# Products of 128x256 pieces: ordered by width in the FFN, and two-column-block products with halves summed in the projections

## The chip, the cores and the metric

The kernel runs on one core of a Trainium2 chip, in one launch. The metric is the device time of that launch in microseconds (us). Before the change it is 1240.27 us, the median of three runs (1240.12 to 1240.30).

## What is computed

The input x is 256 tokens by 1024 features in float32. Two models run one after the other on it, each of depth two:

```
x = x + gmlp_mixer(x);            x = x + swiglu_ffn(x)      # first_block, layer 0
x = x + chunked_attention(x);     x = x + swiglu_ffn(x)      # layer 1: 16 heads, relative bias
x = rms_norm(x)
for l in range(2):                                          # second_block
    p = rms_norm(x) @ w_in[l]                               # 2832 columns
    y = concat(conv31(p), attention4(p), gated_linear_attention(p)) @ w_out[l]
    x = x + y
    u = conv3(rms_norm(x) @ ffn_w_up[l])
    x = x + (silu(u[:, :2816]) * u[:, 2816:]) @ ffn_w_down[l]
x = rms_norm(x)
```

All weights are float32 and are read from memory once. The matrix products are made from pairs of a rounded high part and a low part: a product h @ w is hi(h)·hi(w) + lo(h)·hi(w) + hi(h)·lo(w).

## The kernel before

**Staging.** SP's queue brings the weights in tiles of 128x2048 (`raw`). For each half of such a tile ScalarE (ACT) writes the high part `wh` (L105) and VectorE (DVE) the low part `wl` (L116, or L118 where a gain is multiplied in). `take` hands such pairs to the products in the order of the stream, `release` gives them back, `pump` splits the next ones ahead of their use, up to eight. The activations lie transposed in `hT`, of shape 128 x 8 x 2 x 256: for each of the eight feature blocks k the high part of all 256 tokens and behind it the low part, so that `hT[2][:, k]` is one operand of 512 columns.

**Pieces.** A piece is a product of 128 output features with all 256 tokens: the weight block is the stationary operand, the tokens stream. There are two ways to make one:

- narrow (`mmB`, L350 to L352): 24 products of 256 columns, all into one half of a PSUM bank: for each k wh with hi, wh with lo, wl with hi. `mmB2` makes two pieces into the two halves of one bank. The reader takes the bank directly.
- wide (`mmB_wide`, L363 and L366): eight products of 512 columns (wh with hi and lo side by side, into the two halves of one bank) and eight of 256 columns (wl with hi, into the first half), alternately; the last two change places. The piece is then the sum of the bank's halves: ACT copies the second half out (L634), DVE adds the first (L636).

The four FFNs use the wide form for pieces 2 to 21 of both halves of the up projection (2 x 20 in each FFN). The gMLP groups (16 pieces), the attention's k and q (16), and in each of the two mixers the conv inputs (4), two q/k pairs (4), the gated attention's q (2) and k (2) use the narrow form. The other products are `mmA` (tokens stationary, L339) and `down` (L393 to L395), all 512 columns wide but for one of 272.

**Order.** Only SP's order is written out by hand; on the other engines a scheduler places the instructions of each engine by the program's order and its own estimates, and the order is then fixed. PSUM has eight banks in one pool, of which `down` holds four while it accumulates. In the mixer the 60 taps of the 31-wide convolution (L958, DVE, 128x256 each) are background work: `step` puts a few behind each `pump`. The mixer's `kd` and `kg` (L1063, L1064) are DVE products of the k pieces with decays; PE transposes `kd` (L1080) and multiplies `kg` (L1113) between the products of `gate(0)`. In attention, step s makes k and q of s (`project`, copied out at L858 and L859), and PE's scores (L746) use them one step later, for the first step one product later.

Of the kernel before, what the change touches and what calls it, by code (L numbers as in the profile page):

```python
# [150 lines left out]
class Net:  # L151
# [192 lines left out]
    def mmB(self, out, hT, w):  # L344

        mm = self.nc.tensor.matmul
        vh = w[0].rearrange("p (k n) -> p k n", n=P)
        vl = w[1].rearrange("p (k n) -> p k n", n=P)
        for k in range(KD):
            mm(out, lhsT=vh[:, k, :], rhs=hT[0][:, k, :], start=(k == 0), stop=False)  # L350
            mm(out, lhsT=vh[:, k, :], rhs=hT[1][:, k, :], start=False, stop=False)  # L351
            mm(out, lhsT=vl[:, k, :], rhs=hT[0][:, k, :], start=False, stop=(k == KD - 1))  # L352

    def mmB_wide(self, hT, w):


        mm = self.nc.tensor.matmul
        ps = self.mm([P, 2, S])
        vh = w[0].rearrange("p (k n) -> p k n", n=P)
        vl = w[1].rearrange("p (k n) -> p k n", n=P)  # L360

        def wide(k):
            mm(ps, lhsT=vh[:, k, :], rhs=hT[2][:, k], start=(k == 0), stop=(k == KD - 1))  # L363

        def low(k):
            mm(ps[:, 0, :], lhsT=vl[:, k, :], rhs=hT[0][:, k, :], start=False, stop=False)  # L366

        for k in range(KD):
            for f in (wide, low) if k < KD - 1 else (low, wide):
                f(k)  # L370
        return ps

    def mmB2(self, hT, name="mm"):

        ids, ws = self.ws.take(2)
        ps = self.mm([P, 2, S], name)
        for j in range(2):
            self.mmB(ps[:, j, :], hT, ws[j])
        self.ws.release(ids)
        return ps  # L380
# [239 lines left out]
    def ffn(self, hT, fin, next_gains, conv=None, final=False):  # L620
        nc = self.nc
        with self.tc.tile_pool(name="ff", bufs=1) as pool:
            self.ws.ext(pool, DEFER)
            acts = {}

            wide = True
# [54 lines left out]
            for i in range(2, NPAIR):  # L681
                if wide:
                    ids, ws = self.ws.take(2)
                    ps = [self.mmB_wide(hT, w) for w in ws]
                    self.ws.release(ids)
                else:
                    ps = self.mmB2(hT)
# [101 lines left out]
    def attention(self, hTs, fin, second, next_gains):  # L789
        nc = self.nc  # L790
        hkv, hq = hTs
        with self.tc.tile_pool(name="at", bufs=1) as pool:
# [25 lines left out]
            def project(s, ws, ps, which):  # L818
                self.mmB(ps[:, which, :], (hq, hkv)[which], ws)
# [24 lines left out]
            for s in range(8):  # L844
                ids, ws = self.ws.take(2)
                ps = self.mm([P, 2, S])
                project(s, ws[0], ps, 1)
# [7 lines left out]
                project(s, ws[1], ps, 0)  # L855
                self.ws.release(ids)
                qk = pool.tile([P, 2, S], F32, tag="qk", name="qk", bufs=2)
# [41 lines left out]
    def mixer(self, l, hT, fin, next_gains):  # L899
# [5 lines left out]
        with self.tc.tile_pool(name="mx", bufs=1) as pool:  # L905
# [100 lines left out]
            ids, ws = self.ws.take(2)  # L1006
            ps = self.mm([P, 2, S])
            self.mmB(ps[:, 0, :], hT, ws[0])
            lg = self.mm([P, 2, S], "lg")
            for t in range(2):  # L1010
                nc.tensor.matmul(lg[:, t, :], lhsT=gT[:, t * P : (t + 1) * P], rhs=gw,
                                 start=True, stop=True)
            la = big([P, 2, S], "la")
            last = nc.scalar.activation(la, lg, AF.Abs)
            with self.tc.issue_after(last.ins):
                ld = nc.scalar.preload_act_table_set("natural_log_exp_and_others")
            with self.tc.issue_after(ld.ins):
                nc.scalar.activation(la, la, AF.Exp, scale=-1.0)
            nc.scalar.activation(la, la, AF.Ln, bias=1.0)
            nc.vector.scalar_tensor_tensor(la, lg, 0.0, la, op0=ALU.min, op1=ALU.subtract)  # L1020
            self.mmB(ps[:, 1, :], hT, ws[1])
            self.ws.release(ids)
            qk_out(ps)
            step(2, TAPS[4])
            qk_out(self.mmB2(hT))
# [5 lines left out]
            ids, ws = self.ws.take(2)  # L1031
            qps = self.mm([P, 2, S])
            self.mmB(qps[:, 0, :], hT, ws[0])
            gts = []
            for m in (tri, aft):
                gt = self.mm([P, 2, S], "gt")
                for s in range(2):
                    for t in range(2):
                        nc.tensor.matmul(gt[:, s, t * P : (t + 1) * P],
                                         lhsT=la[:, t, s * P : (s + 1) * P], rhs=m,  # L1040
                                         start=True, stop=True)
                gts.append(gt)
# [3 lines left out]
            nc.scalar.activation(eG, gts[0], AF.Exp)  # L1046
            nc.scalar.activation(enG, gts[0], AF.Exp, scale=-1.0)
            nc.scalar.activation(kdx, gts[1], AF.Exp)
            self.mmB(qps[:, 1, :], hT, ws[1])
            self.ws.release(ids)  # L1050
# [11 lines left out]
            ps = self.mmB2(hT)  # L1062
            nc.vector.tensor_mul(kd, ps, kdx)  # L1063
            nc.vector.tensor_mul(kg, ps, enG)  # L1064
# [437 lines left out]
```

## Time and profile before

| | before |
|---|---|
| median of three runs | 1240.27 us |
| the profiled execution: its time | 1240.27 us |
| the profiled execution: its span | 1238.5 us |
| mean granted TensorE clock | 0.999 of 2.4 GHz |
| TensorE matmul (PE) busy | 1228.8 us, 7160 instructions |
| VectorE (DVE) busy | 903.5 us |
| ScalarE (ACT) busy | 715.1 us |

The span is the time from the first to the last instruction; 1.8 us of the execution lie around it. PE's rows start when a product starts; their ends are modelled, so neighbouring products overlap in the records, and what a product costs in a stream is the distance from its start to the start of the next. PEld is the load of a stationary operand, which runs beside the product ahead of it.

### The profile page before, as it was taken

What the parts mean: (1) busy time and instruction counts of PE and PEld (TensorE: products, weight loads), DVE (VectorE), ACT (ScalarE), POOL (GpSimd) and SP (SyncE); (2) the same over time, 40 slices, a digit from 0 to 9 for tenths busy, and PEclk for the clock granted to TensorE, in tenths of its full rate; (3) what the DMA queues carried; (4) which work ended last, traced back from release to release, by engine and by line L of the source; (5) the groups of instructions that cost most, each with busy time, mean ns of one, the idle gap of its engine ahead of it and who ended that gap; (6) DMA issues with size and microseconds to landing.
All of it is one profiled execution on the core that took longest, in us unless ns stands there. A gap on an engine that the chain in (4) does not pass through costs nothing.

```text
span 1238.5 us, 18456 instructions
## 1 busy us (share of the span) xinstructions
PE 1228.8 (99%) x7160; PEld 1055.0 (85%) x7160; DVE 903.5 (73%) x1497; ACT 715.1 (58%) x1237; POOL 41.3 (3%) x95
## 2 busy tenths in 40 slices
PE   9999999999999999999999999999999999999997
PEld 7899888888888888888889878888888978888886
DVE  6676676766567757676669867979885977889874
ACT  7644465655456546565546556667663745767653
POOL 1100000000000000000010010000001011000000
PEclk9999999999999999999999999999999999999999
DMA  8854465675444435567524345557542425566720
GB/s 290 307 201 170 153 210 199 209 267 192 148 161 171 163 134 206 183 238 246 184 103 170 120 155 203 171 187 278 198 170 86 164 75 216 182 221 216 252 71 34
DMA packets 34827, 226.14 MB, mean 183 GB/s; under 512 B 4242, under 2 KB 4660, under 8 KB 9140
## 3 DMA queue, kind: packets, MB, share of 16 engines
q1 hardware_dynamic: 34596, 224.97, 51.7%
q8 instruction: 56, 0.92, 0.3%
q14 instruction: 31, 0.25, 0.1%
q10 hardware_dynamic: 144, 0.00, 0.0%
HBM read 223.91 MB, written 1.05 MB: 182 GB/s over the span
## 4 chain that ended last, share of the span: by engine, by line
PE 97%; DVE 2%; ACT 1%; POOL 0%; issue 0%; POOLq 0%; ACTq 0%
PE mm L363 24%; PE mm L339 12%; PE mm L366 12%; PE acc L393 9%; PE acc L395 9%; PE acc L394 9%; PE mm L350 5%; PE mm L351 4%; PE mm L352 4%; PE tr L239 1%; PE sc L746 1%; PE mm L497 1%; PE pt L777 1%; PE sp L578 1%; PE po L835 1%; PE po L1202 0%
## 5 line engine op out<-in xcount | busy, mean ns | idle before, releaser
L116 DVE TENSOR_TENSOR wl<-raw,wh 128x1024 fp32r<-128x1024 f32 x378 | 458.8, 1223 | 201.0 <-ACT wh L105 200.1
L105 ACT ACTIVATE wh<-raw 128x1024 fp32r<-128x1024 f32 x378 | 395.1, 1055 | 246.1 <-PE mm L363 89.5
L363 PE MATMUL mm<-hT,wh 128*128 128x512 f32 x1280 | 452.1, 397 | 0.0
L366 PE MATMUL mm<-hT,wl 128*128 128x256 f32 x1280 | 333.2, 281 | 0.0
L363 PEld LDWEIGHTS mm<-hT,wh 128*128 128x128 f32 x1280 | 235.2, 188 | 46.2
L366 PEld LDWEIGHTS mm<-hT,wl 128*128 128x128 f32 x1280 | 241.6, 189 | 14.2
L339 PE MATMUL mm<-wh,hT 128*128 128x512 f32 (+1 forms) x480 | 149.1, 383 | 0.0
L350 PE MATMUL mm<-hT,wh 128*128 128x256 f32 x448 | 128.9, 288 | 0.0
L351 PE MATMUL mm<-hT,wh 128*128 128x256 f32 x448 | 126.8, 283 | 0.1
L352 PE MATMUL mm<-hT,wl 128*128 128x256 f32 x448 | 126.6, 283 | 0.0
L393 PE MATMUL acc<-wh,ah 128*128 128x512 f32 x320 | 125.6, 393 | 0.0
L395 PE MATMUL acc<-wh,al 128*128 128x512 f32 x320 | 124.5, 389 | 0.0
L394 PE MATMUL acc<-wl,ah 128*128 128x512 f32 x320 | 124.5, 389 | 0.0
L339 PEld LDWEIGHTS mm<-wh,hT 128*128 128x128 f32 x480 | 86.8, 188 | 16.8 <-issue 1.1
L350 PEld LDWEIGHTS mm<-hT,wh 128*128 128x128 f32 x448 | 85.7, 191 | 5.5 <-issue 5.2
L339 PE MATMUL mm<-wl,hT 128*128 128x512 f32 (+1 forms) x240 | 90.2, 381 | 0.0
L351 PEld LDWEIGHTS mm<-hT,wh 128*128 128x128 f32 x448 | 85.8, 192 | 0.7 <-DVE hT L233 0.5
L352 PEld LDWEIGHTS mm<-hT,wl 128*128 128x128 f32 x448 | 85.8, 191 | 0.0
L636 DVE TENSOR_TENSOR sum<-mm,sum 128x256 f32<-128x256 f32 x160 | 66.6, 419 | 15.1 <-ACT sum L634 15.0
L651 DVE SCALAR_TENSOR_TENSOR gu<-sum,prm,gu 128x255 f32<-128x255 f32 (+1 forms) x160 | 72.7, 480 | 5.4 <-ACT gu L646 3.5
L634 ACT ACTIVATE sum<-mm 128x256 f32<-128x256 f32 x160 | 58.8, 369 | 31.1 <-PE mm L363 30.7
L394 PEld LDWEIGHTS acc<-wl,ah 128*128 128x128 f32 x320 | 60.2, 188 | 13.0
(221 smaller groups left out, 1458.5 us busy)
## 6 DMA issues: line engine op xcount, KB each, us to landing
raw<-in_w_ffn SPq DMA_DIRECT2D x66, 1024.0 KB, 4.9
raw<-in_w_up SPq DMA_DIRECT2D x66, 1024.0 KB, 4.9
raw<-in_w_mix SPq DMA_DIRECT2D x30, 1024.0 KB, 4.9
raw<-in_w_gmlp SPq DMA_DIRECT2D x22, 1024.0 KB, 5.1
raw<-in_w_att SPq DMA_DIRECT2D x16, 1024.0 KB, 4.9
raw<-in_w_gmlp SPq DMA_DIRECT2D x4, 512.0 KB, 6.2
bias<-in_rel SPq DMA_DIRECT2D x8, 256.0 KB, 3.9
x<-in_x SPq DMA_DIRECT2D x4, 256.0 KB, 5.4
```

What stands on the lines that cost most here:

```text
L105: self.nc.scalar.activation(hi, r, AF.Copy, scale=1.0 if g is None else g)
L116: self.nc.vector.tensor_sub(lo, r, hi.bitcast(F32))
L339: mm(out, lhsT=hT[a][:, k, ts], rhs=view(b, k), start=(i == 0), stop=(i == 3 * KD - 1))
L350: mm(out, lhsT=vh[:, k, :], rhs=hT[0][:, k, :], start=(k == 0), stop=False)
L351: mm(out, lhsT=vh[:, k, :], rhs=hT[1][:, k, :], start=False, stop=False)
L352: mm(out, lhsT=vl[:, k, :], rhs=hT[0][:, k, :], start=False, stop=(k == KD - 1))
L363: mm(ps, lhsT=vh[:, k, :], rhs=hT[2][:, k], start=(k == 0), stop=(k == KD - 1))
L366: mm(ps[:, 0, :], lhsT=vl[:, k, :], rhs=hT[0][:, k, :], start=False, stop=False)
L393: mm(acc, lhsT=act[0][:, ts], rhs=w[0][:, c], start=(first and i == 0), stop=False)
L394: mm(acc, lhsT=act[0][:, ts], rhs=w[1][:, c], start=False, stop=False)
L395: mm(acc, lhsT=act[1][:, ts], rhs=w[0][:, c], start=False, stop=(last and i == n - 1))
L651: nc.vector.scalar_tensor_tensor(gu[:, j, d:], ps[:, j, : S - d], ws3[j][2 - d], gu[:, j, d:], op0=ALU.mult, op1=ALU.add,)
```

## The change

The wide form no longer alternates: it makes seven products of 512 columns, then the eight of 256, then the last of 512. The narrow form and `mmB2` are gone; all 56 pieces that used them are wide now, and two new functions sum the halves into an SBUF tile, with a scale where q is scaled. What read the bank before reads that tile. `qk` in attention has three buffers for two. In the mixers the work that stood between two narrow pieces (`logits`, `decays`) is passed as `mid` and stands at the same place.

```diff
     def mmB_wide(self, hT, w):
-        for k in range(KD):
-            for f in (wide, low) if k < KD - 1 else (low, wide):
-                f(k)
+        for k in range(KD - 1):
+            wide(k)
+        for k in range(KD):
+            low(k)
+        wide(KD - 1)
         return ps
 
-    def mmB2(self, hT, name="mm"):
+    def half_sum(self, ps, out, scale=1.0):
+        self.nc.scalar.activation(out, ps[:, 1, :], AF.Copy, scale=scale)
+        if scale == 1.0:
+            self.nc.vector.tensor_add(out, ps[:, 0, :], out)
+        else:
+            self.nc.vector.scalar_tensor_tensor(out, ps[:, 0, :], scale, out,
+                                                op0=ALU.mult, op1=ALU.add)
+
+    def mmB_sum(self, hT, outs, scales=(1.0, 1.0), mid=None):
         ids, ws = self.ws.take(2)
-        ps = self.mm([P, 2, S], name)
         for j in range(2):
-            self.mmB(ps[:, j, :], hT, ws[j])
+            if j == 1 and mid is not None:
+                mid()
+            self.half_sum(self.mmB_wide(hT, ws[j]), outs[j], scales[j])
         self.ws.release(ids)
...
# gMLP, group(g)
-                ps = self.mmB2(hT)
-                nc.vector.tensor_mul(u, ps, rrow[:, None, :].to_broadcast([P, 2, S]))
+                self.mmB_sum(hT, [u[:, j, :] for j in range(2)])
+                nc.vector.tensor_mul(u, u, rrow[:, None, :].to_broadcast([P, 2, S]))
...
# attention, step s
-            def project(s, ws, ps, which):
-                self.mmB(ps[:, which, :], (hq, hkv)[which], ws)
+            def project(ws, qk, which):
+                self.half_sum(self.mmB_wide((hq, hkv)[which], ws), qk[:, which, :],
+                              (0.125, 1.0)[which])
...
-                nc.scalar.activation(qk[:, 0, :], ps[:, 0, :], AF.Copy, scale=0.125)
-                nc.vector.tensor_copy(qk[:, 1, :], ps[:, 1, :])
...
# mixer
             def conv_in(s):
-                ps = self.mmB2(hT)
-                nc.scalar.activation(th, ps[:, 1, :], AF.Tanh, scale=0.5)
-                nc.vector.scalar_tensor_tensor(hpad[:, s, 30:], th, 1.0, ps[:, 0, :],
-                                               op0=ALU.add, op1=ALU.mult)
+                c = hpad[:, s, 30:]
+                self.mmB_sum(hT, [c, th])
+                nc.scalar.activation(th, th, AF.Tanh, scale=0.5)
+                nc.vector.scalar_tensor_tensor(c, th, 1.0, c, op0=ALU.add, op1=ALU.mult)
...
-            def qk_out(ps):
+            def qk_out(mid=None):
                 qk = big([P, 2, S], "qk")
-                nc.scalar.activation(qk[:, 0, :], ps[:, 0, :], AF.Copy, scale=0.125)
-                nc.scalar.activation(qk[:, 1, :], ps[:, 1, :], AF.Copy)
+                self.mmB_sum(hT, [qk[:, j, :] for j in range(2)], (0.125, 1.0), mid)
...
-            nc.vector.scalar_tensor_tensor(qg, qps, 0.125, eG, op0=ALU.mult, op1=ALU.mult)
+            self.mmB_sum(hT, [qg[:, j, :] for j in range(2)], (0.125, 0.125), decays)
+            nc.vector.tensor_mul(qg, qg, eG)
...
-            ps = self.mmB2(hT)
-            nc.vector.tensor_mul(kd, ps, kdx)
-            nc.vector.tensor_mul(kg, ps, enG)
+            self.mmB_sum(hT, [kg[:, j, :] for j in range(2)])
+            nc.vector.tensor_mul(kd, kg, kdx)
+            nc.vector.tensor_mul(kg, kg, enG)
```

How the instructions stand on their engines is shown at three places. In each row stand the line, the operation, what is written and read, the shape, and a count where a row repeats.

The first place is PE in the first FFN, behind the `down` products of a step: two pieces. Before (L363 is the wide product, L366 the low one):

```order
L395 MATMUL acc_1717<-wh,al 128x512
L363 MATMUL mm<-hT,wh 128x512
L366 MATMUL mm<-hT,wl 128x256
L363 MATMUL mm<-hT,wh 128x512
L366 MATMUL mm<-hT,wl 128x256
L363 MATMUL mm<-hT,wh 128x512
L366 MATMUL mm<-hT,wl 128x256 x2
L363 MATMUL mm<-hT,wh 128x512 x2
L366 MATMUL mm<-hT,wl 128x256
```

After the change (L354 is the wide product, L357 the low one, L397 the last of `down`):

```order
L397 MATMUL acc_1629<-wh,al 128x512
L354 MATMUL mm<-hT,wh 128x512 x7
L357 MATMUL mm<-hT,wl 128x256 x8
L354 MATMUL mm<-hT,wh 128x512 x8
L357 MATMUL mm<-hT,wl 128x256 x8
L354 MATMUL mm<-hT,wh 128x512
```

The widths change fourteen times inside a piece before and twice after; the last wide product of the first piece joins the seven of the second.

The second place is DVE in the first mixer, around `kd` and `kg` (L958 and L953 are the taps, L370 the sum of halves). Before:

```order
L958 SCALAR_TENSOR_TENSOR cy<-hpad,prm,cy 128x256 x2
L116 TENSOR_TENSOR wl<-raw,wh 128x1024
L958 SCALAR_TENSOR_TENSOR cy<-hpad,prm,cy 128x256 x2
L118 SCALAR_TENSOR_TENSOR wl<-raw,misc,wh 128x1024
L958 SCALAR_TENSOR_TENSOR cy<-hpad,prm,cy 128x256 x2
L1063 TENSOR_TENSOR kd<-mm,kdx 128x512
L1064 TENSOR_TENSOR kg<-mm,enG 128x512
```

After:

```order
L953 SCALAR_TENSOR_TENSOR cy<-hpad,prm,cy 128x256 x4
L116 TENSOR_TENSOR wl<-raw,wh 128x1024
L370 TENSOR_TENSOR kg<-mm,kg 128x256
L953 SCALAR_TENSOR_TENSOR cy<-hpad,prm,cy 128x256 x2
L116 TENSOR_TENSOR wl<-raw,wh 128x1024
L370 TENSOR_TENSOR kg<-mm,kg 128x256
L953 SCALAR_TENSOR_TENSOR cy<-hpad,prm,cy 128x256
L1054 TENSOR_TENSOR kd<-kg,kdx 128x512
L953 SCALAR_TENSOR_TENSOR cy<-hpad,prm,cy 128x256
L1055 TENSOR_TENSOR kg<-kg,enG 128x512
L118 SCALAR_TENSOR_TENSOR wl<-raw,misc,wh 128x1024
```

Two sums now stand ahead of `kd` here, and the last gained split has moved behind `kg`. From the second conv gate (L966 before, L962 after) to `kg` there are on DVE 51 taps and 12 splits before, and 50 taps, 11 splits and eight sums after.

The third place is PE at the start of the first mixer, where the first conv piece needs the last part of `hT` (names with their buffer numbers; `mm_6160` is the first conv piece before, `mm_5969` after). Before:

```order
L239 MATMUL tr_6146<-ident_101,hn_6098 128x128 x4
L339 MATMUL mm_6117<-wh_5904,hT_6038 128x512
L350 MATMUL mm_6160<-hT_6038,wh_5907 128x256
L350 MATMUL mm_6224<-hT_6038,wh_6213 128x256
L351 MATMUL mm_6160<-hT_6038,wh_5907 128x256
L352 MATMUL mm_6160<-hT_6038,wl_5908 128x256
```

After:

```order
L239 MATMUL tr_5954<-ident_101,hn_5906 128x128 x4
L339 MATMUL mm_5925<-wh_5712,hT_5846 128x512
L354 MATMUL mm_5969<-hT_5846,wh_5715 128x512 x4
L354 MATMUL mm_5988<-hT_5846,wh_5745 128x512
L354 MATMUL mm_5969<-hT_5846,wh_5715 128x512 x3
L357 MATMUL mm_5969<-hT_5846,wl_5716 128x256 x8
```

Two products that read the high part alone stood first; now the first product reads high and low parts together.

## Rows read from the trace of the kernel before

**Rows 1.** The page: busy us, share and instructions of each engine; the chain's shares.
```profile
PE 1228.8 (99%) x7160; PEld 1055.0 (85%) x7160; DVE 903.5 (73%) x1497; ACT 715.1 (58%) x1237; POOL 41.3 (3%) x95
...
PE 97%; DVE 2%; ACT 1%; POOL 0%; issue 0%; POOLq 0%; ACTq 0%
```

**Rows 2.** Waits of PE, the longest: waiter, releaser, us in total, times, longest.
```profile
PE warm L423 <- POOL ident masks.py:199: 1.4, 1, 1.4
```

**Rows 3.** Groups by line: count | busy us, mean ns | idle before.
```profile
L363 PE MATMUL mm<-hT,wh 128*128 128x512 f32 x1280 | 452.1, 397 | 0.0
...
L350 PE MATMUL mm<-hT,wh 128*128 128x256 f32 x448 | 128.9, 288 | 0.0
```

**Rows 4.** Timeline of PE, first FFN: start us, duration us, line, operands, count.
```profile
295.57 0.39 PE L363 MATMUL mm<-hT,wh 128*128 128x512 f32 x1
...
300.97 0.40 PE L363 MATMUL mm<-hT,wh 128*128 128x512 f32 x1
301.21 0.40 PE L393 MATMUL acc<-wh,ah 128*128 128x512 f32 x1
...
301.67 0.39 PE L395 MATMUL acc<-wh,al 128*128 128x512 f32 x1
...
303.93 0.39 PE L363 MATMUL mm<-hT,wh 128*128 128x512 f32 x1
```

**Rows 5.** Timeline of PE, a gMLP group: first narrow product, and what follows 48.
```profile
79.39 0.28 PE L350 MATMUL mm<-hT,wh 128*128 128x256 f32 x1
...
85.14 0.72 PE L578 MATMUL sp<-wsT,v 128*128 128x128 f32 x5
```

**Rows 6.** Timeline of PE, first mixer: 512-column products behind a run of 272.
```profile
664.18 0.40 PE L339 MATMUL mm<-wl,hT 128*128 128x512 f32 x1
...
666.03 0.39 PE L339 MATMUL mm<-wl,hT 128*128 128x512 f32 x1
```

**Rows 7.** Groups by line: a weight split, and the two steps of a sum.
```profile
L116 DVE TENSOR_TENSOR wl<-raw,wh 128x1024 fp32r<-128x1024 f32 x378 | 458.8, 1223 | 201.0 <-ACT wh L105 200.1
...
L636 DVE TENSOR_TENSOR sum<-mm,sum 128x256 f32<-128x256 f32 x160 | 66.6, 419 | 15.1 <-ACT sum L634 15.0
...
L634 ACT ACTIVATE sum<-mm 128x256 f32<-128x256 f32 x160 | 58.8, 369 | 31.1 <-PE mm L363 30.7
```

**Rows 8.** Busy us by stretch: length, then PE, PEld, DVE, ACT, POOL.
```profile
53.00:152.00 99.00, 99.00 (x656) 90.95 (x656) 66.59 (x78) 47.11 (x61) 1.95 (x5) 1.00 0.52 180
361.00:426.00 65.00, 65.00 (x539) 58.68 (x538) 48.74 (x138) 41.54 (x99) 1.59 (x8) 1.00 0.50 180
...
655.00:705.00 50.00, 50.00 (x373) 46.04 (x373) 48.95 (x104) 32.83 (x59) 0.00 (x0) 1.00 0.50 170
```

**Rows 9.** Tile uvh, gMLP: durations min/median/max ns, first and last start.
```profile
L393 PE MATMUL acc<-wh,uvh x64: 389/389/477, 73.8 to 151.1; 128*128 128x512 f32 x64
...
L232 ACT ACTIVATE uvh<-u x8: 631/633/634, 64.7 to 137.2; 128x512 fp32r<-128x512 f32 x8
```

**Rows 10.** Timeline of all engines, first mixer: the first conv piece and its wait.
```profile
645.80 0.69 DVE L233 TENSOR_TENSOR hT<-tr,hT 128x512 fp32r<-128x512 f32 x1
...
646.10 0.40 PE L350 MATMUL mm<-hT,wh 128*128 128x256 f32 x2
646.54 0.19 PEld L351 LDWEIGHTS mm<-hT,wh 128*128 128x128 f32 x1 [0.26 <-DVE hT L233]
```

**Rows 11.** Timelines of DVE and PE, attention: first step's copy, and its scores.
```profile
370.63 0.42 DVE L859 COPY qk<-mm 128x256 f32<-128x256 f32 x1
...
371.28 0.49 PE L746 MATMUL sc<-qk 64*128 64x128 f32 x4
```

**Rows 12.** Timeline of DVE, first mixer: eleven taps, and kg.
```profile
660.67 4.57 DVE L958 SCALAR_TENSOR_TENSOR cy<-hpad,prm,cy 128x256 f32<-128x256 f32 x11
...
698.70 0.70 DVE L1064 TENSOR_TENSOR kg<-mm,enG 128x512 f32<-128x512 f32 x1
```

**Rows 13.** Timeline of PE, first mixer: where kg is first read.
```profile
703.07 0.72 PE L1113 MATMUL at<-qg,kg 64*128 64x128 f32 x8
```

More of the change, by code (lines that the diff above doesn't have):

```diff
@@ L342, in mmA @@
                     f()
[L344 to L348, printed above, removed]
-        for k in range(KD):
-            mm(out, lhsT=vh[:, k, :], rhs=hT[0][:, k, :], start=(k == 0), stop=False)
-            mm(out, lhsT=vh[:, k, :], rhs=hT[1][:, k, :], start=False, stop=False)
-            mm(out, lhsT=vl[:, k, :], rhs=hT[0][:, k, :], start=False, stop=(k == KD - 1))
     def mmB_wide(self, hT, w):
@@ L624, in ffn @@
             acts = {}
-            wide = True
             def finish(i, ps):
@@ L681, in ffn @@
             for i in range(2, NPAIR):
[L682 to L686, printed above, removed]
-                    ps = self.mmB2(hT)
+                ids, ws = self.ws.take(2)
+                ps = [self.mmB_wide(hT, w) for w in ws]
+                self.ws.release(ids)
                 if i == 2:
@@ L845, in attention @@
                 ids, ws = self.ws.take(2)
-                ps = self.mm([P, 2, S])
-                project(s, ws[0], ps, 1)
+                qk = pool.tile([P, 2, S], F32, tag="qk", name="qk", bufs=3)
+                project(ws[0], qk, 1)
                 if s >= 2:
@@ L854, in attention @@
                     load_bias(s + 3)
-                project(s, ws[1], ps, 0)
+                project(ws[1], qk, 0)
                 self.ws.release(ids)
-                qk = pool.tile([P, 2, S], F32, tag="qk", name="qk", bufs=2)
-                nc.scalar.activation(qk[:, 0, :], ps[:, 0, :], AF.Copy, scale=0.125)
-                nc.vector.tensor_copy(qk[:, 1, :], ps[:, 1, :])
                 qks[s] = qk
@@ L998, in mixer @@
             qks = []
-            def qk_out(ps):
+            def qk_out(mid=None):
                 qk = big([P, 2, S], "qk")
-                nc.scalar.activation(qk[:, 0, :], ps[:, 0, :], AF.Copy, scale=0.125)
-                nc.scalar.activation(qk[:, 1, :], ps[:, 1, :], AF.Copy)
+                self.mmB_sum(hT, [qk[:, j, :] for j in range(2)], (0.125, 1.0), mid)
                 qks.append(qk)
-            ids, ws = self.ws.take(2)
-            ps = self.mm([P, 2, S])
-            self.mmB(ps[:, 0, :], hT, ws[0])
@@ L1009, in mixer @@
[L1009 to L1012, printed above, removed]
-            la = big([P, 2, S], "la")
[L1014 to L1023, printed above, removed]
+            la = big([P, 2, S], "la")
+            def logits():
+                lg = self.mm([P, 2, S], "lg")
+                for t in range(2):
+                    nc.tensor.matmul(lg[:, t, :], lhsT=gT[:, t * P : (t + 1) * P], rhs=gw,
+                                     start=True, stop=True)
+                last = nc.scalar.activation(la, lg, AF.Abs)
+                with self.tc.issue_after(last.ins):
+                    ld = nc.scalar.preload_act_table_set("natural_log_exp_and_others")
+                with self.tc.issue_after(ld.ins):
+                    nc.scalar.activation(la, la, AF.Exp, scale=-1.0)
+                nc.scalar.activation(la, la, AF.Ln, bias=1.0)
+                nc.vector.scalar_tensor_tensor(la, lg, 0.0, la, op0=ALU.min, op1=ALU.subtract)
@@ L1024, in mixer @@
+            qk_out(logits)
             step(2, TAPS[4])
-            qk_out(self.mmB2(hT))
+            qk_out()
             sm0, sums0 = self.sm_scores(pool, qks[0], [caus, caus], False, 4)
             step(2, TAPS[5])
[L1031 to L1042, printed above, removed]
@@ L1045, in mixer, with decays @@
             kdx = big([P, 2, S], "kdx")
[L1046 to L1050, printed above, removed]
+            def decays():
+                gts = []
+                for m in (tri, aft):
+                    gt = self.mm([P, 2, S], "gt")
+                    for s in range(2):
+                        for t in range(2):
+                            nc.tensor.matmul(gt[:, s, t * P : (t + 1) * P],
+                                             lhsT=la[:, t, s * P : (s + 1) * P], rhs=m,
+                                             start=True, stop=True)
+                    gts.append(gt)
+                nc.scalar.activation(eG, gts[0], AF.Exp)
+                nc.scalar.activation(enG, gts[0], AF.Exp, scale=-1.0)
+                nc.scalar.activation(kdx, gts[1], AF.Exp)
             qg = big([P, 2, S], "qg")
+            self.mmB_sum(hT, [qg[:, j, :] for j in range(2)], (0.125, 0.125), decays)
             kg = big([P, 2, S], "kg")
             kd = big([P, 2, S], "kd")
-            nc.vector.scalar_tensor_tensor(qg, qps, 0.125, eG, op0=ALU.mult, op1=ALU.mult)
+            nc.vector.tensor_mul(qg, qg, eG)
             sm1, sums1 = self.sm_scores(pool, qks[1], [caus, caus], False, 4)
```

2 lines of the change are left out of this document (removed).

## The prediction, made before the change was run

> **What bounds the kernel now.** I began with the page: PE is busy for 1228.8 us of a span of 1238.5 and makes 97% of the chain, while DVE and ACT work 73% and 58% of the span [rows 1]. The view of waits then has PE's largest wait, 1.4 us, at the warm-up at the start; the others come to less than 2 us together [rows 2]. So PE is the bound from one end to the other, and at full clock (mean granted clock 0.999 of 2.4 GHz). The time can only fall if the same products take PE less time, and it can only rise if PE begins to wait. Busy sums don't show the first, since their durations (397 ns for a product of 512 columns, 288 for one of 256, [rows 3]) overlap. What counts is the distance from one start to the next, and for that I read the timeline of PE.
>
> - A stream of 512: from 301.67 to 303.93 lie ten products of `down`, 2.26 us, 226 ns each [rows 4].
> - A stream of 256: 48 products in 79.39 to 85.14, 5.75 us, 119.8 ns each. That is a pair of narrow pieces, so one narrow piece is 2.875 us [rows 5].
> - The alternating piece: two of them run from 295.57 to 301.21, so one is 2.82 us [rows 4].
>
> Eight products of 512 and eight of 256 at their streams' distances would be 8 x 0.226 + 8 x 0.1198 = 2.766 us. The alternating piece thus pays about 0.054 us for its fourteen changes of width, and the narrow one pays 0.109 us for having 24 products where 16 would do. These two excesses are all that the change can win.
>
> **The piece after the change.** It has two changes of width, and the eight wide products come in one run behind each run of eight low ones. What remains of the 0.054 us has to be bounded. If each change costs alike, 2/14 of it stays: 0.007 us, a piece of 2.773. But the rows say that a run of 512 starts slowly behind narrower products: the three from 300.97 to 301.67, which follow two low products, take 0.70 us where 3 x 0.226 is 0.678, so 0.022 more [rows 4]; and in the first mixer eight products of 512 behind a run of 272-column ones take 1.85 us where 8 x 0.226 is 1.808, 0.042 more [rows 6]. Ends: 0.007 and 0.042. I take 0.022, because those rows hold the very products of this piece, a wide one behind low ones. The piece is then 2.788 us, between 2.773 and 2.808.
>
> **The FFNs.** 1280 wide products by eight are 160 pieces [rows 3]. Each gains 2.82 − 2.788 = 0.032 us: 5.1 us, with ends of 1.9 (0.012 each) and 7.5 (0.047 each). No engine gets more work there, and the sums come at the same place.
>
> **The projections.** 448 products in L350, by eight, are 56 narrow pieces [rows 3]. Each gains 2.875 − 2.788 = 0.087 us: 4.9 us, with ends of 3.8 (0.067) and 5.7 (0.102).
>
> The Trainium skill, on its page "TensorE: Matmul & The Clock Gate", section "Back-to-back issue gap", gives for isolated products one cycle of 2.4 GHz per column and a fixed 2.5 ns: 216 ns for 512 columns and 109 for 256. By it order is worth nothing, and dropping eight of 24 products saves 20 ns a piece, 1.1 us in all as an estimate. The trace differs, with 226 and 119.8 ns [rows 4, 5], and the measurement decides.
>
> **What the sums add.** Each of the 56 pieces now needs a copy on ACT, 0.369 us, and a sum on DVE, 0.419 us [rows 7]. Eight sums take the place of copies, so DVE gets 48 x 0.42 = 20 us and ACT, where 16 copies fall away, 40 x 0.37 = 15 us. Both are off PE's path as long as they have room: in the gMLP DVE works 66.6 of 99 us, in the attention 48.7 of 65 [rows 8]. In the gMLP the gated product is written from 64.7 on and first read by `down` at 73.8 [rows 9]; a cover of 8 us and more hides a sum of 0.8 us. Cost nothing; with the cover gone it would be those 0.8 us once per group. The gMLP's other `take`s and the queues of SP and POOL keep their rows, so no transfer moves.
>
> **Three places where a reader is close behind.**
>
> First, the start of each mixer. DVE writes the last low part of `hT` at 645.80; PE makes two products that need only the high part at 646.10, and the next, which needs the low one, starts at 646.54 [rows 10]. The first wide product needs both, so the two products, 0.24 us at 119.8 each, no longer fill the wait. Twice: 0.5 us. The ends are 0 (something else fills it) and 1.4 (the write comes later by its own length, 0.69 us, in either mixer).
>
> Second, attention's first step: DVE's copy of k starts at 370.63, and the scores start at 371.28 [rows 11]. The copy's place is taken by ACT's copy and DVE's sum, 0.79 for 0.42, while the one or two pieces ahead of it end 0.087 us earlier each. I take 0.1 us; the ends are 0 and one split of 1.2 [rows 7], if one queues ahead. The other steps read a whole step later and hide it.
>
> Third, `kd` and `kg` in the mixers, where DVE has no idle time: 48.95 us of 50 busy [rows 8]. What stands ahead of `kg` changes from 51 taps and 12 splits to 50 taps, 11 splits and eight sums. A tap is 4.57 / 11 = 0.42 us [rows 12], a split 1.22 [rows 7]: 8 x 0.42 − 0.42 − 1.22 = 1.72 us later. `kg` starts at 698.70 and takes 0.70 [rows 12], so it would end at 701.1. PE first reads it at 703.07 [rows 13]; twelve projection pieces ahead of it gain 12 x 0.087 and the first place gives 0.24 back, so PE wants it at 702.3. That leaves 1.2 us of the 3.7 there are now. Cost 0; as it stands close, the end is 1.4 per mixer, a split and a bit more than the slack taken away.
>
> **The sum.** 5.1 + 4.9 − 0.5 − 0.1 = 9.4 us. The profiled execution itself took 1240.27 us, which is the median of the three runs: 1240.27 − 9.4 = 1230.9. I say 1231.0.
>
> **The rivals.**
>
> *The run-in costs its full price.* Each run of wide products behind low ones costs 0.042 us as behind the 272s [rows 6]. Then the FFNs win 1.9 and the projections 3.8, less 0.6: 1235.2 us. For it: those are eight products in a row, as many as a run after the change. Against: the narrower products there are another line and another width. Chance 0.12.
>
> *DVE becomes the bound in front of `kg`.* If DVE is more than 1.2 us later than worked out, by a split more ahead of `kd`, PE waits for `kg`, and each us beyond costs one in either mixer. Up to two splits, 2.4 us, twice: up to 1236, some 1233.5 in the middle. For it: DVE has hardly a gap there [rows 8]. Against: taps can step back, and the rows were counted in the order itself. Chance 0.09.
>
> *Columns alone count.* All forms have 6144 columns a piece: eight by 512 and eight by 256, or 24 by 256. If PE's time went by columns, nothing would be won and 0.6 us lost: 1240.9. Against it: 226 / 512 is 0.441 ns a column, 119.8 / 256 is 0.468 [rows 4, 5]; and the two forms differ by 0.055 us a piece. Chance 0.02. The page named above comes near to this with a time of about 1239.8, as an estimate.
>
> *Banks come back late: slower.* A wide piece takes a bank of its own, where a pair of narrow ones shared one, and it is free only when ACT has copied and DVE has summed. In the attention a step then uses seven banks of the eight where it used six. If a sum stands behind a split, the bank is held 0.37 + 1.22 + 0.42 = 2.0 us longer [rows 7]. Should PE wait that long in each of the eight steps, it loses 16 us, and the time is 1247; with the first five of them the gain is gone. For it: DVE is 75% busy in this stage [rows 8]. Against: the FFNs give banks back in just this way for 160 pieces, and no wait of PE there reaches 1.4 us [rows 2]. Chance 0.04.
>
> That the change doesn't do what it says is nearly excluded, as the order of PE has seven, eight and one in the FFN and in the mixer.
>
> **How the numbers follow.** The forecast has 0.73, the four rivals 0.12, 0.09, 0.02 and 0.04. The range: below, both gains at their upper ends, 7.5 + 5.7 − 0.6 = 12.6, 1227.7 us; above, the run-in at its full price, 1235.2, set at 1235.4 for what the first place may cost more; it takes in most of the second rival. Outside lie the last two rivals, the worst of the second and a few hundredths below. About 0.2%, 2.5 us, is what a measurement of this kernel can tell from no change, so faster means below 1237.8. The forecast and the first two rivals are faster, 0.94, less 0.01 for a sum of misfortunes: 0.93. The same is 0.03 (columns alone, and the edge of the last rival), slower 0.04.
>
> **What the profile after would show.** The FFN: two pieces from the first wide product to the first of `down` in 5.58 us for 5.64, with the 0.022 in the first two or three wide products of each run; if two pieces take 5.62, the first rival holds. The projections: a pair in 5.58 us for 5.75. PE's waits: new rows of 0.2 to 0.3 us at the first conv piece, for `hT` from DVE; a row at `kg` (L1104 or near) for the second rival; a row at a wide product of the attention, for a bank freed by a sum, for the last. DVE's load between 655 and 705 stays full and ACT's rises. The prediction is wrong if the wide products in runs are not at 226 ns, or if PE's waits grow past 3 us.

## The result and the profile after

The changed kernel takes 1233.22 us, the median of six runs (1232.45 to 1233.95), against 1240.14 for the kernel before, measured beside it (1240.12 to 1240.30, six runs). The ratio is 0.9944 with a 95% interval of 0.9934 to 0.9954: 6.9 us less, where 9.4 were forecast. The profiled execution took 1232.47 us, at the lower edge of the six; against the profiled execution of before it is 7.8 us shorter. So two things are to be explained: 1.6 us between the gain that was forecast and the gain of this execution, and another 0.75 between this execution and the median. The second has its own sign: the times of before lie within 0.2 us, those of the changed kernel within 1.5.

The page of the changed kernel, its first part, answers to [rows 1]; below it PE's waits, which answer to [rows 2] (engine and line, what it waited for, us in total, times, longest):

```profile
PE 1220.2 (99%) x6712; PEld 1031.3 (84%) x6712; DVE 918.9 (75%) x1545; ACT 727.6 (59%) x1277; POOL 41.6 (3%) x95
```

```profile
PE warm L425 <- POOL ident masks.py:199: 1.4, 1, 1.4
PE mm L499 <- DVE wl L116: 0.9, 2, 0.5
PE mm L354 <- DVE hT L233: 0.6, 2, 0.3
PE tr L239 <- DMA x<-in_x: 0.3, 1, 0.3
PE tr L239 <- DVE hn L221: 0.3, 1, 0.3
PE acc L395 <- ACT ah L232: 0.2, 1, 0.2
```

PE is still the bound: 8.6 us less busy, 448 products fewer, DVE 15.4 and ACT 12.5 us more. One row is new, the first wide product of each mixer behind `hT`, 0.3 us twice, as the prediction said. No wait for a bank in the attention and none at `kd` or `kg` is to be seen in this execution. One sign failed: between 655 and 705 us DVE stays full (49.55 of 50 us), but ACT's load did not rise (32.30 us for 32.83; the same stretch, with a mixer that begins 4.6 us earlier).

The timeline of PE in the first FFN and in a gMLP group (start, duration, line, operands, count) answers to [rows 4] and [rows 5]; L395 to L397 are `down`:

```profile
293.33 1.75 PE L354 MATMUL mm<-hT,wh 128*128 128x512 f32 x7
294.92 1.11 PE L357 MATMUL mm<-hT,wl 128*128 128x256 f32 x8
295.87 2.00 PE L354 MATMUL mm<-hT,wh 128*128 128x512 f32 x8
297.71 1.12 PE L357 MATMUL mm<-hT,wl 128*128 128x256 f32 x8
298.67 0.40 PE L354 MATMUL mm<-hT,wh 128*128 128x512 f32 x1
298.90 0.40 PE L395 MATMUL acc<-wh,ah 128*128 128x512 f32 x1
...
301.64 1.07 PE L354 MATMUL mm<-hT,wh 128*128 128x512 f32 x4
```

```profile
78.90 1.75 PE L354 MATMUL mm<-hT,wh 128*128 128x512 f32 x7
...
84.47 1.05 PE L580 MATMUL sp<-wsT,v 128*128 128x128 f32 x8
```

Two FFN pieces take 298.90 - 293.33 = 5.57 us, for 5.64 before; but the twelve `down` products behind them take 301.64 - 298.90 = 2.74, for 2.72 before (301.21 to 303.93 in [rows 4]). A pair of pieces with its `down` thus went from 8.36 to 8.31; the means over 72 such pairs, by the nanosecond starts in the traces, are 8.363 and 8.313. A pair in the gMLP takes 5.57 us, for 5.75.

The same product of PE, looked up in both timelines at the border of each stage, gives what every stage won, in us (a worked table, not rows of a view):

```
stage          gMLP  FFN 1  attention  FFN 2  mixer 1  FFN 3  mixer 2  FFN 4  sum
expected       1.4   1.3    1.3        1.3    0.8      1.3    0.8      1.3    9.4
measured       1.5   1.0    1.1        1.0    0.6      1.1    0.65     1.05   8.0
```

The four FFNs gave 4.1 us for the 5.1 expected, the projections 3.9 for 4.3; 0.2 of the 8.0 is given back in the tail behind the last product.

### The profile page after: what moved, and what is told of

The parts are those of the page before. It is cut to its first block, busy times and chain, and to the rows that moved or that the text cites. A ratio compares the mean times of both kernels' runs of the same rounds, so it can differ in the third digit from the quotient of the medians.

```text
span 1230.7 us, 17579 instructions
## 1 busy us (share of the span) xinstructions
PE 1220.2 (99%) x6712; PEld 1031.3 (84%) x6712; DVE 918.9 (75%) x1545; ACT 727.6 (59%) x1277; POOL 41.6 (3%) x95
## 4 chain that ended last, share of the span: by engine, by line
PE 97%; DVE 2%; ACT 1%; POOL 0%; issue 0%; POOLq 0%; ACTq 0%
PE mm L354 32%; PE mm L357 17%; PE mm L339 12%; PE acc L395 9%; PE acc L397 9%; PE acc L396 9%; PE tr L239 1%; PE sc L743 1%; PE mm L499 1%; PE pt L774 1%; PE sp L580 1%; PE po L833 1%; PE po L1193 0%; PE dS L1081 0%; PE po L1189 0%; ACT sq L196 0%
## 5 line engine op out<-in xcount | busy, mean ns | idle before, releaser
L354 PE MATMUL mm<-hT,wh 128*128 128x512 f32 x1728 | 452.7, 393 | 0.6 <-DVE hT L233 0.6
L354 PEld LDWEIGHTS mm<-hT,wh 128*128 128x128 f32 x1728 | 315.9, 189 | 61.9 <-issue 5.2
L357 PEld LDWEIGHTS mm<-hT,wl 128*128 128x128 f32 x1728 | 235.7, 190 | 17.0
L357 PE MATMUL mm<-hT,wl 128*128 128x256 f32 x1728 | 240.9, 282 | 0.0
L395 PE MATMUL acc<-wh,ah 128*128 128x512 f32 x320 | 126.0, 394 | 0.0
L397 PE MATMUL acc<-wh,al 128*128 128x512 f32 x320 | 124.9, 390 | 0.0
L397 PEld LDWEIGHTS acc<-wh,al 128*128 128x128 f32 x320 | 60.1, 188 | 13.5
L395 PEld LDWEIGHTS acc<-wh,ah 128*128 128x128 f32 x320 | 60.4, 189 | 10.0 <-issue 0.3
L646 ACT ACTIVATE gu<-sum,prm 128x256 f32<-128x256 f32 x80 | 46.5, 594 | 19.9 <-DVE sum L636 19.9
L339 PEld LDWEIGHTS mm<-wl,hT 128*128 128x128 f32 x240 | 45.1, 188 | 9.3 <-issue 1.1
L953 DVE SCALAR_TENSOR_TENSOR cy<-hpad,prm,cy 128x256 f32<-128x256 f32 x120 | 52.0, 485 | 0.3
L660 ACT ACTIVATE sg<-sum 128x256 f32<-128x256 f32 x40 | 16.6, 416 | 40.8 <-DVE sum L636 40.8
```

The costliest lines, as they stand in the source:

```text
L339: mm(out, lhsT=hT[a][:, k, ts], rhs=view(b, k), start=(i == 0), stop=(i == 3 * KD - 1))
L395: mm(acc, lhsT=act[0][:, ts], rhs=w[0][:, c], start=(first and i == 0), stop=False)
L397: mm(acc, lhsT=act[1][:, ts], rhs=w[0][:, c], start=False, stop=(last and i == n - 1))
L953: nc.vector.scalar_tensor_tensor(y[:, s, :], hpad[:, s, j : j + S], prm[:, w : w + 1], y[:, s, :], op0=ALU.mult, op1=ALU.add)
```

## The experiments

**Control.** The changed kernel once more.

> The changed kernel once more. Its six times so far lie between 1232.45 and 1233.95 us, while the six of the kernel before lie within 0.2 us; the profiled one of them, 1232.47, is at the lower edge. Theory: the spread of 1.5 us is at some place that only some executions pass through, so the median stays near 1233.2 and the lowest near 1232.4; if the profile of this run is one of the longer ones, the distance between its products and those of the first profile shows the place. Rival: the spread is of that one chip or session, and the times here agree within 0.3 us.

Five runs: 1232.54 median, 1232.32 to 1234.03, ratio 0.9942 (0.9929 to 0.9954). The spread is there again, and this run's profile fell on a short execution.

**The order alone.** The kernel before with

```diff
-        for k in range(KD):
-            for f in (wide, low) if k < KD - 1 else (low, wide):
-                f(k)
+        for k in range(KD - 1):
+            wide(k)
+        for k in range(KD):
+            low(k)
+        wide(KD - 1)
```

> Only the order in the FFN's 160 wide pieces is changed; the 56 narrow pieces stay as before. Theory: a run of wide products behind low ones costs 27 ns more than its stream, of which the first low products behind it give 7 back, so an ordered piece takes 2.793 us and gains 0.027: 4.3 us, a time of 1235.9 (1235.4 to 1236.3). An FFN step of six pieces and two groups of down goes from 25.08 to 24.92 us. Rival, the prediction's 0.032 a piece: 5.1 us, 1235.1, and a step of 24.89. Rival, only columns count: 1240.2.

1236.08 us (1236.01 to 1236.13), ratio 0.9968 (0.9955 to 0.9980): a gain of 4.0 us, no spread. That is 80 pairs by the 0.05 us of the timeline, and it is well below the 5.1 of the prediction. The expectation's own term, 0.027 us a piece or 4.3 us, was a little high too.

**The sums alone.** The changed kernel, but its FFN makes its pieces with a copy of the alternating function of before:

```diff
...
-                ps = [self.mmB_wide(hT, w) for w in ws]
+                ps = [self.mmB_alt(hT, w) for w in ws]
```

> Only the 56 projection pieces become wide ones with sums, in the new order; the FFN alternates as before. Theory: 0.087 us a piece, 4.9, less 0.6 at the start of each mixer and of the attention: a gain of 4.2, a time of about 1236.0 (1235.5 to 1236.8), with no wait of PE but two of about 0.3 us for hT in the mixers. The gains of this run and of the run with the order alone add up to that of the whole change. Rival, DVE late for kg: a wait of PE at the line that reads kg and a gain under 3.

1236.79 us median of eight runs, 1236.46 to 1238.11, ratio 0.9974 (0.9963 to 0.9984). By the shortest execution the gain is 3.6 us, and 4.0 + 3.6 = 7.6 is what the changed kernel wins in its own short executions (7.5 to 7.8): the two parts add up. By the median it is 3.3. The spread of 1.65 us comes with this part. The execution that was profiled is the longest, 1238.11, and it has a wait of PE at `kg`, as the rival expected, and one at `kd`, in the first mixer. Waits of PE in that stretch:

```profile
PE tr L1088 <- DVE kd L1071: 0.5, 1, 0.5
PE at L1121 <- ACT wh L105: 0.4, 1, 0.4
```

Its timelines of ACT and DVE there (in brackets the idle time before, and what ended it):

```profile
692.97 1.15 ACT L105 ACTIVATE wh<-raw,misc 128x1024 fp32r<-128x1024 f32 x1 [2.69 <-DMA raw<-in_w_mix]
...
695.40 0.36 ACT L385 ACTIVATE kg<-mm 128x256 f32<-128x256 f32 x1
```

```profile
695.79 0.42 DVE L387 TENSOR_TENSOR kg<-mm,kg 128x256 f32<-128x256 f32 x1 [1.82 <-ACT kg L385]
...
699.17 0.68 DVE L1071 TENSOR_TENSOR kd<-kg,kdx 128x512 f32<-128x512 f32 x1
```

Read from the top: ACT stands for 2.69 us at a weight split whose tile has not landed. The copy of the first k piece's half is behind it, comes at 695.40, and DVE, idle for 1.82 us, can sum only then. So `kd` is late, and PE waits. Set beside the control's starts from the beginning of the mixer on, PE falls behind by 0.62 us at `kd`, 0.56 at `kg` and 0.34 at a product further on that reads the state which DVE updates (L1210): 1.5 us in this mixer, of the 1.65 by which the execution is longer than the shortest. The view names a split of ACT as what ended the wait at L1121; what that product reads is `kg`, which DVE writes right behind `kd`.

**A look for a long execution of the changed kernel itself**, three single runs of it.

> The changed kernel, one execution with its profile. Theory: an execution over 1233 us shows in the first or second mixer a weight tile that lands late, ACT waiting over 2 us for it with the copy of a k piece's half behind it, and PE waiting for kd and at kg for what is over 1.2 us of that; one under 1232.8 shows no such wait. Rival: a long execution has its extra time elsewhere.

> The same as the run before it: if over 1233 us, the extra time stands at kd and kg in a mixer; if under 1232.8, nowhere.

> The same again: if over 1233 us, the extra time stands at kd and kg in a mixer; if under 1232.8, nowhere.

They took 1232.99, 1232.49 and 1232.38 us. The first is half a us longer than the second, and its products stand level with those of the control's short execution from the first products on (within 0.05 us, and 0.02 in the first mixer) until PE comes to `kg` there. There they part. ACT in the control and then in the long one, the same split and the same copy:

```profile
688.52 1.15 ACT L105 ACTIVATE wh<-raw,misc 128x1024 fp32r<-128x1024 f32 x1 [0.35 <-DMA raw<-in_w_mix]
...
690.95 0.36 ACT L368 ACTIVATE kg<-mm 128x256 f32<-128x256 f32 x1
```

```profile
689.85 1.15 ACT L105 ACTIVATE wh<-raw,misc 128x1024 fp32r<-128x1024 f32 x1 [1.67 <-DMA raw<-in_w_mix]
...
692.27 0.36 ACT L368 ACTIVATE kg<-mm 128x256 f32<-128x256 f32 x1
```

and `kg` on DVE with its first reader on PE, in the control:

```profile
695.75 0.70 DVE L1055 TENSOR_TENSOR kg<-kg,enG 128x512 f32<-128x512 f32 x1
```

```profile
697.71 0.72 PE L1104 MATMUL at<-qg,kg 64*128 64x128 f32 x8
```

and in the long one:

```profile
697.05 0.68 DVE L1055 TENSOR_TENSOR kg<-kg,enG 128x512 f32<-128x512 f32 x1
```

```profile
697.88 0.71 PE L1104 MATMUL at<-qg,kg 64*128 64x128 f32 x8
...
713.41 0.95 PE L1193 MATMUL po<-state,qg 64*32 64x128 f32 x8
```

The tile is 1.3 us later, the copy 1.3, `kg` 1.3, and PE 0.17: the rest, 1.1 us, was slack (in the control `kg` ends at 696.45 and is read at 697.71). DVE stays behind by half a us, and at L1193, which reads the state that DVE updates, PE loses the other 0.34 (those eight products take 0.95 for 0.60 in the control). The expectation had ACT waiting over 2 us for the tile and PE waiting for `kd` too, in an execution over 1233 us. This one, 1232.99, lies just under that mark; ACT waited 1.67 us, `kd` was still in time, and the second place was not foreseen. That the extra time begins at the late tile in the mixer held. The two short ones fit: their tile came no more than 0.4 us later than the control's, which the slack covers, and PE loses nothing at `kd` and `kg`.

**The k pieces narrow again**, in the changed kernel (`mmB` and `mmB2` are as before):

```diff
...
-            self.mmB_sum(hT, [kg[:, j, :] for j in range(2)])
-            nc.vector.tensor_mul(kd, kg, kdx)
-            nc.vector.tensor_mul(kg, kg, enG)
+            ps = self.mmB2(hT)
+            nc.vector.tensor_mul(kd, ps, kdx)
+            nc.vector.tensor_mul(kg, ps, enG)
```

> The changed kernel with the mixers' gated k pieces (two a mixer) narrow again, kd and kg reading the bank directly. The profile of a long execution of sums_only (1238.11 us) has PE waiting 0.48 us for kd and 0.43 at kg in the first mixer, because ACT stood 2.69 us at a weight split whose tile had not landed, with the copy of a k piece's half behind it. Theory: that queue is what makes the changed kernel's times spread from 1232.3 to 1234.0. Without those copies a late tile no longer reaches kd: the times agree within 0.4 us, at 1232.4 + 4 x 0.087 = 1232.8 us. Rival: the spread is elsewhere, and about half of the executions stay over 1233.2, up to 1234.3.

1232.72 us, all five within 1232.66 to 1232.85, ratio 0.9940 (0.9928 to 0.9953). The spread is gone for 0.3 us of gain given up; the medians of the changed kernel are 1233.22 and 1232.54. In its profile `kg` ends at 694.93 and is read at 697.80, 2.9 us later. No tile was late in the profiled execution, so that a late one is harmless here follows from the order of the engines and was not seen.

**The slack alone taken away**, in the kernel before:

```diff
-            nc.vector.tensor_mul(kd, ps, kdx)
+            for _ in range(4):
+                nc.vector.tensor_mul(kd, ps, kdx)
```

> The kernel before, with kd written four times in place of once: three more products of 0.6 us and a tap ahead of kg take 2.5 of the 3.7 us by which kg was early, so that DVE's slack is that of the changed kernel, about 1.2 us, but nothing of the k pieces goes through ACT. Theory (ACT's queue behind a late tile): no effect, 1240.1 us, all times within 0.4 us. Rival (the small slack on DVE alone lets any jitter through): a spread of a us or more, 1240.1 to 1241.6. Rival (the slack is not there): every execution is slower by 1 us or more in either mixer, 1242 and over.

```profile
701.29 0.68 DVE L1065 TENSOR_TENSOR kg<-mm,enG 128x512 f32<-128x512 f32 x1
```

```profile
703.14 0.71 PE L1114 MATMUL at<-qg,kg 64*128 64x128 f32 x8
```

`kg` now ends at 701.97 and is read at 703.14: 1.2 us of slack, as in the changed kernel. The time is 1240.11 (eleven runs, 1239.94 to 1240.51), ratio 1.0000 (0.9991 to 1.0009). So the small slack on DVE by itself costs nothing and brings no spread. What the run doesn't test is that slack together with a late tile. ACT at the same split:

```profile
691.13 1.15 ACT L105 ACTIVATE wh<-raw,misc 128x1024 fp32r<-128x1024 f32 x1 [2.04 <-PE mm L351]
```

Here the split waits for PE to give a buffer back, and its tile had landed at 689.07, 2.06 us ahead of it: a tile 1.3 us late would still have been in time. In the kernel before it is the same (landed 689.14, split 691.06). In the changed kernel the split waits for the tile itself in each of the five profiled executions, 0.20 to 0.70 us in the four short ones. The transfer has moved: SP issues it when DVE has made the low part that frees a `raw` buffer, in the kernel before 47.5 us after the first product of the mixer (684.51 behind 637.00), in the control 51.3 (683.66 behind 632.35). So the changed kernel has not only put the copy behind that split; its tile also comes 3.8 us later in the stage. That the sums on DVE, which has no idle time there, make the low part late is argued from DVE's order; no run takes it apart.

**Longer runs.** Where two pieces follow each other, all wide products of both come first:

```diff
...
+        for ps, w in zip(pss, v):
+            for k in range(KD):
+                mm(ps, lhsT=w[0][:, k, :], rhs=hT[2][:, k], start=(k == 0), stop=False)
+        for ps, w in zip(pss, v):
+            for k in range(KD):
+                mm(ps[:, 0, :], lhsT=w[1][:, k, :], rhs=hT[0][:, k, :], start=False, stop=(k == KD - 1))
...
```

> The changed kernel, but where two pieces follow each other (80 pairs in the FFNs, 8 in the gMLP, 8 in the mixers) all 16 wide products of both come first and then the 16 low ones: one run-in a pair for two. Theory: 96 x 0.020 = 1.9 us less than the changed kernel, about 1231.3, and a pair in 5.54 us where the changed kernel has 5.57. Rival: the price hangs on the number of products behind each change (a longer run pays more), and the time is that of the changed kernel within 0.5 us. Rival: both sums at the end of a pair make their readers late, with new waits of PE, and it is slower by 1 us or more.

1230.73 us (1230.68 to 1230.99), ratio 0.9925 (0.9912 to 0.9937): 1.7 us under the short executions of the changed kernel, 2.5 under its median. PE in the first FFN:

```profile
292.90 3.79 PE L372 MATMUL mm<-hT,wh 128*128 128x512 f32 x16
296.53 2.08 PE L375 MATMUL mm<-hT,wl 128*128 128x256 f32 x16
298.44 0.40 PE L409 MATMUL acc<-wh,ah 128*128 128x512 f32 x1
```

Sixteen wide products behind the 512 columns of `down` take 3.63 us, 226.7 ns each by the nanosecond starts, with no run-in; in the changed kernel eight of them behind low ones take 297.71 - 295.87 = 1.84, 27 ns more than 8 x 226.7. Sixteen low ones take 1.91, 119.4 each. One run-in less a pair, 96 pairs: 1.7 / 96 = 0.018 us each. The runs also agree within 0.3 us, though a late tile could hold up `kd` here as well; five runs don't show that it can't.

**The high parts first**, on top of that, for the first conv piece of each mixer:

```diff
...
+        for h in range(2):
+            for k in range(hi):
+                mm(pss[0][:, h, :], lhsT=v[0][0][:, k, :], rhs=hT[h][:, k, :], start=(h + k == 0), stop=False)
...
-                self.mmB_sum(hT, [c, th])
+                self.mmB_sum(hT, [c, th], hi=0 if s else 2)
```

> The grouped kernel (1230.73 us), but the first conv piece of each mixer begins with the high parts of two feature blocks as products of 256 columns, then their low parts, then the wide products. Theory: the two high products fill 0.24 us of the wait for the last low part of hT, and four narrow products cost 0.027 more than two wide ones: 2 x 0.21 = 0.4 us less, 1230.3, and the waits of PE for hT at the conv piece (0.3 us twice) fall to under 0.1 each. Rival: the wait moves to the low products or to the other pieces and the time stays at 1230.7.

1230.18 us (1230.10 to 1230.21), ratio 0.9919 (0.9906 to 0.9933), 0.55 us less. First the grouped kernel at the start of the first mixer, then this one:

```profile
641.00 1.19 PE L372 MATMUL mm<-hT,wh 128*128 128x512 f32 x4 [0.28 <-DVE hT L233]
```

```profile
640.37 0.95 PE L372 MATMUL mm<-hT,wh 128*128 128x256 f32 x4
641.16 1.08 PE L375 MATMUL mm<-hT,wh 128*128 128x512 f32 x4
```

The wait for `hT` is out of the view of waits. This is the best version found: 9.9 us under the kernel before, 3.0 under the changed kernel.

**The old order everywhere**, in the changed kernel (the order of the diff above taken back, in all 216 wide pieces):

> The changed kernel with the old alternating order in all of its 216 wide pieces. Theory: the FFN is as before, and a projection piece gains 2.88 - 2.8175 = 0.062 us: 3.5, less 0.6 at the readers: 1237.2 us for fast executions (up to 1.5 more where kd is late). Against the run with the sums and the new order in the projections (1236.46 at its lowest) it is 0.7 to 1.4 us slower. Rival, that order is worth nothing where DVE and ACT are busy: as that run, 1236.5.

1237.45 us, ten of eleven runs within 1237.37 to 1237.54 and one at 1238.87; ratio 0.9980 (0.9971 to 0.9988). It is 0.9 us over the short executions of the sums alone, which differ from it in the order of the 56 projection pieces: 0.016 us a piece, somewhat below the FFN's 0.025.

This run also bears on the spread. It keeps the copies of the k pieces on ACT, its slack at `kg` is the same (1.29 us in the profile), and its split waits for the tile (0.30 us), yet one execution in eleven is long. Counted as more than 0.35 us over the shortest of their kernel, 7 of 14 executions of the changed kernel are long, 4 of 8 of the sums alone, 1 of 11 here, and none of 9 of the two kernels with longer runs, which keep the copies too. What sets how often a tile is late was not found, and the five even times with narrow k pieces are therefore weak evidence alone; the two profiles of long executions carry the argument.

## Why the prediction was right or wrong

**PE as the bound, and the distances between starts: right.** The gain came from where the two excesses were seen, the parts add up, and no other stage moved.

**The FFN's 5.1 us: the mechanism right, the size wrong.** The term that failed is the price of the ordered piece, 2.788 us. Its floor was put together from 226 and 119.8 ns, each worked out from two starts of a timeline with two decimals; the streams run at 226.67 (sixteen products in 3.627 us) and 120.0, which makes the floor 8 x 0.22667 + 8 x 0.120 = 2.773 where the prediction had 2.766. The run-in, taken as 0.022 from three products behind two low ones (0.016 by the nanosecond starts), is 0.027 over five products behind eight, of which the low run gives 0.007 back (its first products come sooner): 0.020. That is 2.793 by its parts; a whole pair cost 8.31 - 2.72 = 5.59, or 2.795 a piece. So the gain is 0.025 x 160 = 4.0, as measured.

Where the prediction looked, it seems right: a pair up to the first `down` was to take 5.58 us and takes 5.57, 0.064 less than before. That is in part luck, since the low floor and the run-in that was charged in full to both runs cancel there. Most of the second run-in falls into `down`: its twelve products take 2.741 us for 2.727 (means over the same 72 pairs), and 80 times 0.0134 is the 1.1 us that was missing. The bounds, 1.9 and 7.5, held. The first rival did not come about: the 0.042 behind the 272s is not the price behind low products.

**The projections' 4.9 us: nearly right.** In the gMLP a pair fell from 5.75 to 5.57, 0.09 a piece for 0.087. The attention gave 1.1 for 1.3 and the mixers 0.6 for 0.8. There wide pieces often stand behind products of 64 to 256 columns and pay the run-in that a narrow piece doesn't; that is argued, no run here takes it apart.

**The start of the mixers: right.** 0.3 us twice in the view of waits, and 0.55 us back when the wait is filled with high parts again.

**The sums beside PE: right in the gMLP and the attention**, where PE has no new wait, so the fourth rival (banks) did not come about. **In the mixers the step failed that said cost 0.** The slack was right: 1.2 us worked out, 1.26 measured in the control between the end of `kg` and its reader. What was not in the working is ACT and the transfers. The rows ahead of `kd` were counted on DVE only; but each k piece now also passes through a copy on ACT, and that copy stands behind a weight split that begins when its tile lands. In the profile of before that tile landed 1.9 us ahead of its split; in the changed kernel its transfer starts 3.8 us later in the stage, and the split stands waiting for it. The prediction kept the transfers in place for the gMLP and did not ask about them in the mixers. In the first profiled execution of the changed kernel the tile landed only 0.1 us behind the control's, so the price was 0 in it. A tile 1.3 us late cost 0.5 us, one 2.3 us late (2.69 for 0.35) some 1.5, 1.2 of it at `kd` and `kg`. This is the second rival's place with another cause, one that acts in some executions and not in others. It would account for the median's last 0.75 us. Two long executions were profiled, one of the changed kernel and one of the sums alone, and both show it; that the other long ones have the same cause is not shown.

**Columns alone, the third rival, is out:** order by itself won 4.0 us in the FFNs, and dropping eight products of 24 won 2.7 in the old order (1237.45 for 1240.11) and 3.6 in the new one. The section "Back-to-back issue gap" of the Trainium skill's page "TensorE: Matmul & The Clock Gate" gives 216 and 109 ns for isolated products; the trace differs, with 226.7 and 120.0 in streams in which each product has a weight load of its own.

The time thus came out 2.2 us over the forecast: about 1.0 by the run-in and the rounding in the FFNs, 0.4 in the projections, 0.2 in the tail and 0.75 between the profiled execution and the median, less some 0.13 by which the forecast was rounded up (1230.87 to 1231.0).

## What to carry to other kernels

When a gain is a small difference between two distances, take each from the longest stream that the trace has, and close the balance at the next operation that runs at its steady distance, not at the last instruction of the piece. Put products of one width into runs as long as the banks allow. When a result is led through one more engine, look at what that engine queues ahead of it: behind an instruction that waits for a transfer the result inherits the jitter of that transfer, and the slack to its reader must cover more than one profile shows. When an engine without idle time gets more work, look also at the transfers that wait for it: they start later, and what was early may become just in time.

## What was not expected of the hardware

A run of 512-column products behind 256-column ones starts slowly over five products, not one. In the changed kernel's first FFN their mean distances are 233, 236, 228, 233 and 231 ns before they settle at 227 (means over 39 runs of the nanosecond starts). The first 256-column product behind a 512-column one takes 113 ns and the second 119 before the next settle at 120 (means over 40 runs). The length of the run ahead matters: in the kernel before, behind two products of 256 (the place of [rows 4] and its like), the first three take 236, 233 and 227, 16 ns over the stream for 27 (means over 76 places).

The late tile is late by its end alone, and by one share of sixteen. Busy us in stretches of the transfer of that 1 MB (stretch and its length, then PE, PEld, DVE, ACT and POOL, the granted clock, the share of the DMA engines, GB/s), in the control:

```profile
685.66:687.66 2.00, 2.00 (x14) 1.32 (x13) 2.00 (x6) 0.38 (x1) 0.00 (x0) 1.00 0.95 401
687.66:688.66 1.00, 1.00 (x7) 0.83 (x6) 1.00 (x4) 0.63 (x3) 0.00 (x0) 1.00 0.09 33
688.66:690.66 2.00, 2.00 (x14) 1.78 (x13) 2.00 (x9) 2.00 (x6) 0.00 (x0) 1.00 0.00 0
```

and in the long execution of the changed kernel:

```profile
685.67:687.67 2.00, 2.00 (x14) 1.32 (x13) 2.00 (x6) 0.38 (x1) 0.00 (x0) 1.00 0.93 381
687.67:688.67 1.00, 1.00 (x7) 0.83 (x6) 1.00 (x4) 0.50 (x2) 0.00 (x0) 1.00 0.16 57
688.67:690.67 2.00, 2.00 (x14) 1.78 (x13) 2.00 (x9) 0.82 (x1) 0.00 (x0) 1.00 0.02 8
```

Both have moved nearly all of it by 687.7; in the last stretch of the second only two packets of 8 KB start. The packets in the trace show why. The transfer is 128 packets of 8 KB in sixteen streams of eight, each packet starting where the one before it ends, most of them 0.31 us long, and the split starts 0.3 us behind the last stream. In the control the streams end by 688.20. In the long execution fifteen end by 688.37; in the sixteenth two packets took 0.93 and 0.62 us, and the four behind them end at 689.53. In the profiled execution of the sums alone fifteen streams end by 690.15 and the sixteenth, with two packets of 1.33 and 0.91, at 692.66. Packets of over 0.9 us are no rarity (946 of 25255 packets of 8 KB between 20 and 1200 us in the control, 963 in the long execution). Why two of one stream took so long here was not found.
